# FFN layer two: outer product P7 as seven inner products, its weight differences made in layer one's first half

## The chip, the cores and the metric

One NeuronCore of a Trainium2 chip runs the whole decoder block in one launch. The metric is the device time of the launch in microseconds (us). A launch of this kernel takes about 1.9 ms; the spread of three launches was 1.7 us. Inputs and output are float32. The engines of the core are TensorE (PE in the profile), VectorE (DVE), ScalarE (ACT), GpSimd (POOL) and SyncE (SP). SP does no arithmetic here: it issues nearly all DMA transfers, one after the other, and a transfer that has to wait for its data or for a free buffer keeps those behind it from being issued.

## The reference

Only the FFN bears on the change. 2048 tokens of width 1024 go through two matrices with a squared ReLU between them:

```python
hn2 = rmsnorm(h, norm2_g)
up = jnp.einsum('bsd,df->bsf', hn2, w_up)      # 2048 x 1024 by 1024 x 4096
act = jnp.square(jax.nn.relu(up))
h = h + jnp.einsum('bsf,fd->bsd', act, w_down) # 2048 x 4096 by 4096 x 1024
return rmsnorm(h, final_g)
```

## The kernel before

**Numbers.** Operands are float32. Each one is split into a high part of type fp32r and the rest, also fp32r (`split`, L146 and L147: a copy on ACT, a subtraction on DVE), and each product is three matmuls: high by high, high by low, low by high.

**Strassen products.** Both FFN layers multiply 2x2 blocks by seven block products instead of eight (Winograd's form of Strassen's method). The seven products are called P1 to P7. Their left operands are the activations A11, A12, A22 and the sums S1 to S4 (`S3 = A11 - A21`); their right operands are weight blocks or differences of them. The four token tiles of 512 form two pairs, `PAIRS`, with index `q` 0 and 1; a product is made for both pairs.

**Layer one** (`up`) walks through 32 columns `(q, m)`, numbered 0 to 31 here: 0 to 15 are `q = 0` (the first half), 16 to 31 `q = 1`. Each column has seven slots, one for each product, of 12 matmuls (L1082), in the order P2, P6, P5, P7, P1 of the next column, P4, P3. For each slot a weight tile `hw` is split, four slots ahead of its use (`UA = 4`). The first of these needs, per column, four differences of up-weights (L919 to L922). Behind each slot, `post` evacuates the PSUM bank: it makes the activations on ACT and DVE, the sums S1 to S4 on DVE, and stores each tile to DRAM (`sd`). At column 16 the left operands of the second token pair are loaded and split, 14 tiles `sa` of 128x1024.

**Layer two** (`down`) takes the products in the order P1, P6, P7, P4, P5, P2, P3. P1, P6, P7 and P3 are outer products: eight steps over the inner dimension, each with a weight tile `wd` and one row tile `ad` per pair (L1422). P4, P5 and P2 are listed in `SPLIT`: each is itself made by seven inner products of four steps (L1249), with the two token pairs, the two halves of the inner dimension and the two halves of the columns as its 2x2 blocks. An inner step is 12 matmuls and needs one row tile; two steps share one weight tile. The rows and weights of the inner products are sums and differences:

- the row sums (`sdi`) of A22, S1 and A12 are made in layer one's second half by `inner_row` and `inner_sums`: with column `m` the row of pair 0 is loaded and subtracted, with column `m + 8` the other three sums are made (L885 to L894);
- the weight differences (`wi`) of S1 are made by the generator `weights_first` in layer one's first half: each of its 16 steps loads two quarter tiles of `w_down`, and at the next call subtracts one from the other (L988), stores the difference (`td`), and makes and stores the inner differences (L993), one per step on average. Its calls (`next(first_weights, None)`) stand in the loop over slots;
- those of A12 and A22 are made in layer two, during P1 and P7 (`more_weights`, `inner_weights`, L1137).

The tiles of `post`, of the inner sums and of `weights_first` come from one pool, `avp`, of 13 buffers of 128x512. A buffer is free again when the store that reads it has landed.

**Order.** Each engine works strictly through its own list. The code gives the dependences; the order of the list is set when the program is built, by the framework's scheduler, so that instructions of different columns are interleaved.

Of the kernel before, what the change touches and what calls it, by code (L numbers as in the profile page):

```python
# [15 lines left out]
P = 128  # L16
# [30 lines left out]
def hymba_block(ctx: ExitStack, tc: tile.TileContext, xT, gains, w_in, pool_w, w_out, w_up, w_down, out):  # L47
# [64 lines left out]
    for i in range(PAD):  # L112
# [24 lines left out]
    sdi = {i: [[dram.tile([P, 2, T], F32, name=f"sdi{i}_{n}_{c}") for c in range(4)] for n in range(4)] for i in (1, 2, 3)}  # L137
    wi = {i: {n: [dram.tile([P, 4, 256], F32, name=f"wi{i}_{n}_{c}") for c in range(2)]
              for n in ("P5", "P6", "P7", "P4")} for i in (1, 2, 3)}
    td = [[dram.tile([P, 4, 256], F32, name=f"td{i}_{c}") for c in range(8)] for i in range(2)]  # L140
# [720 lines left out]
    def up(pools, more):  # L861
# [5 lines left out]

        def inner_row(m, i):
# [10 lines left out]
        def inner_sums(m, i, t):  # L879

            rows, at = halves[i, "rows"], m % (NM // 2)
            d, r = rows[0], rows[-1]
# [96 lines left out]
        def weights_first():  # L979

            for k in range(4):
                b = {}
                for x, y in ((0, 0), (0, 1), (1, 1), (1, 0)):
                    b[x, y], t = (avp.tile([P, 2, 256], F32, tag="av", name=n) for n in ("t1", "b11"))
                    nc.sync.dma_start(t, half(w_down[0, k + 4 * x], y))
                    nc.sync.dma_start(b[x, y], half(w_down[1, k + 4 * x], y))
                    yield
                    nc.vector.tensor_tensor(b[x, y], b[x, y], t, ALU.subtract)  # L988
                    nc.sync.dma_start(half(td[0][k + 4 * x], y), b[x, y])
                    for to, one, two, p in {(0, 1): (((0, 0), (0, 1), (0, 0), "P5"),),  # L990
                                            (1, 1): (((0, 1), (1, 1), (0, 1), "P7"), ((1, 1), (1, 1), (0, 0), "P6")),
                                            (1, 0): (((1, 0), (1, 0), (1, 1), "P4"),)}.get((x, y), ()):
                        nc.vector.tensor_tensor(b[to], b[one], b[two], ALU.subtract)  # L993
                        nc.sync.dma_start(wi[S1][p][k // 2][:, 2 * (k % 2):2 * (k % 2) + 2], b[to])

        def post(q, m, s):
# [4 lines left out]
            def put(i, t, kept=None):  # L1001
                if q == 0 or m >= NM // 2 or i not in (A12, A22, S1):
                    kept = nc.sync.dma_start(sd[q][i][m // 2][:, m % 2], t)
                if q and i in (A12, A22, S1):
                    inner_sums(m, i, t)
                return kept
# [17 lines left out]
            elif s == "P6":  # L1024
                if q:
                    for i in (A22, S1, A12):
                        inner_row(m, i)
                copy("u2")
            elif s == "P7":
                copy("u3")  # L1030
# [15 lines left out]
            elif s == "P3":  # L1046
# [6 lines left out]
                put(S4, s4)  # L1053

# [13 lines left out]
        for g, (q, m, s) in enumerate(slots):  # L1068
# [4 lines left out]
            if q == 0 and (m in (1, 6, 7) or m >= NM // 2 and m % (NM // 2) not in (2, 3, 4, 5)) and s in SUMS:  # L1073
# [24 lines left out]
    def down(pools):  # L1098
        t8, s8, rs, rt, pupa, pup, rtx, rlp, tmp_, psb = pools

        SPLIT = {"P4": A22, "P5": S1, "P2": A12}
# [25 lines left out]
        source, tops = {"P4": "t2", "P5": "t1", "P2": 2}, {}  # L1127
# [21 lines left out]
        def more_weights(n, kk, w):  # L1149
# [28 lines left out]
        def make(g):  # L1178
# [11 lines left out]
            elif n == "P7":  # L1190
                w = minus(blk(b22, kk), blk(b12, kk))
# [19 lines left out]
        CHAIN = {"P1": "p1", "P6": "u2", "P7": "u3"}  # L1211
        BANKS = {"P4": {"Y": (0, 1), "Z": (2, 3), "X": (4, 5)}, "P5": {"Y": (6, 7), "Z": (2, 3), "X": (4, 5)},
# [401 lines left out]
```

## Time and profile before

| | us |
|---|---|
| median of three launches | 1913.86 (1912.65 to 1914.35) |
| profiled launch, its own time | 1917.71 |
| span of its profile | 1915.9 |
| layer one, its matmuls | about 697 to 1312 |
| layer two, its matmuls | 1312 to 1905 |

The span runs from the first to the last instruction in the trace. The profiled launch was 3.85 us above the median, and 1.8 us of it lie outside the span. "Busy" counts an engine as busy while at least one of its instructions runs; neighbours on DVE overlap a little, so a DVE operation of 128x512 that shows 0.69 us starts 0.60 us after the one before it. In a table of waits, the name on the right is what ended the wait.

### The profile page before, as it was taken

What the parts mean: (1) busy time and instruction counts of PE and PEld (TensorE: products, weight loads), DVE (VectorE), ACT (ScalarE), POOL (GpSimd) and SP (SyncE); (2) the same over time, 40 slices, a digit from 0 to 9 for tenths busy, and PEclk for the clock granted to TensorE, in tenths of its full rate; (3) what the DMA queues carried; (4) which work ended last, traced back from release to release, by engine and by line L of the source; (5) the groups of instructions that cost most, each with busy time, mean ns of one, the idle gap of its engine ahead of it and who ended that gap; (6) DMA issues with size and microseconds to landing.
All of it is one profiled execution on the core that took longest, in us unless ns stands there. A gap on an engine that the chain in (4) does not pass through costs nothing.

```text
span 1915.9 us, 26510 instructions
## 1 busy us (share of the span) xinstructions
PE 1891.8 (99%) x8995; PEld 1577.8 (82%) x8995; DVE 1424.4 (74%) x2128; ACT 1006.7 (53%) x1598; POOL 177.7 (9%) x399
## 2 busy tenths in 40 slices
PE   9999999999999999999999999999999999999997
PEld 7888888888888888788888888887888888888886
DVE  6887799667866886776787877786655547888874
ACT  5565566555554465455566555454333345656643
POOL 0211113101211030000000000000010010020120
PEclk9999999999999999999999999999999999999998
DMA  6686596787887867776777677778998889899862
GB/s 213 204 270 201 191 295 221 244 312 264 283 321 295 282 239 252 261 254 227 273 285 269 233 258 262 243 266 310 379 358 308 282 253 314 291 297 334 295 209 91
DMA packets 206034, 509.68 MB, mean 266 GB/s; under 512 B 24256, under 2 KB 30400, under 8 KB 202048
## 3 DMA queue, kind: packets, MB, share of 16 engines
q1 hardware_dynamic: 201136, 499.24, 75.1%
q0 software_dynamic: 4608, 8.39, 2.4%
q8 instruction: 73, 1.20, 0.3%
q14 instruction: 73, 0.60, 0.1%
q10 hardware_dynamic: 144, 0.26, 0.0%
HBM read 335.82 MB, written 171.97 MB: 265 GB/s over the span
## 4 chain that ended last, share of the span: by engine, by line
PE 89%; DMA 4%; DVE 4%; issue 1%; ACT 1%; POOL 0%; SPq 0%; DVEq 0%; ACTq 0%
PE pY L1082 16%; PE pb L1422 16%; PE pb L1249 12%; PE pZ L1082 8%; PE pd L178 8%; PE pd L180 8%; PE pd L179 8%; PE pX L1082 4%; PE po L675 2%; PE pta L664 1%; DMA xt<-in_xT_dram 1%; PE pr L231 1%; DMA t<-in_w_down_dram 1%; PE pm L205 1%; PE pz L617 1%; DMA wr<-in_w_down_dram 1%
## 5 line engine op out<-in xcount | busy, mean ns | idle before, releaser
L1082 PE MATMUL pY<-sa,hw 128*128 128x512 f32 x1536 | 365.7, 389 | 0.7 <-ACT u L1015 0.7
L1422 PE MATMUL pb<-ad,wd 128*128 128x512 f32 x1488 | 340.9, 390 | 1.3 <-ACT ad L146 1.2
L1082 PEld LDWEIGHTS pY<-sa,hw 128*128 128x128 f32 x1536 | 288.1, 188 | 60.9 <-ACT u L1015 1.1
L1422 PEld LDWEIGHTS pb<-ad,wd 128*128 128x128 f32 x1488 | 278.5, 188 | 60.0 <-ACT ad L146 1.6
L178 PE MATMUL pd<-h,hl 128*128 128x512 f32 x752 | 299.8, 399 | 0.7 <-DVE qkr L424 0.7
L180 PE MATMUL pd<-h,hl 128*128 128x512 f32 x752 | 296.9, 395 | 0.0
L179 PE MATMUL pd<-h,hl 128*128 128x512 f32 x752 | 296.7, 395 | 0.0
L147 DVE TENSOR_TENSOR ad<-ar,ad 128x1024 fp32r<-128x1024 f32 x148 | 179.8, 1221 | 70.2 <-ACT ad L146 70.0
L1249 PE MATMUL pb<-ad,wd 128*128 128x512 f32 x1008 | 229.2, 389 | 0.5 <-DVE ad L147 0.5
L1249 PEld LDWEIGHTS pb<-ad,wd 128*128 128x128 f32 x1008 | 189.0, 188 | 40.4 <-DVE ad L147 1.2
L146 ACT ACTIVATE ad<-ar 128x1024 fp32r<-128x1024 f32 x148 | 155.6, 1053 | 116.8 <-issue 47.6
L1082 PE MATMUL pZ<-sa,hw 128*128 128x512 f32 x768 | 186.7, 390 | 1.5 <-DVE a L1032 1.5
L1082 PEld LDWEIGHTS pZ<-sa,hw 128*128 128x128 f32 x768 | 143.9, 188 | 32.2 <-DVE a L1032 2.4
L178 PEld LDWEIGHTS pd<-h,hl 128*128 128x128 f32 x752 | 142.1, 189 | 28.2 <-DVE qkr L424 1.0
L180 PEld LDWEIGHTS pd<-h,hl 128*128 128x128 f32 x752 | 141.8, 189 | 28.0
L179 PEld LDWEIGHTS pd<-h,hl 128*128 128x128 f32 x752 | 142.0, 189 | 27.1
L146 ACT ACTIVATE hl<-raw 128x512 fp32r<-128x512 f32 x168 | 104.0, 631 | 111.2 <-PE pd L180 70.7
L147 DVE TENSOR_TENSOR hl<-raw,hl 128x512 fp32r<-128x512 f32 x168 | 114.1, 685 | 53.6 <-ACT hl L146 50.0
L147 DVE TENSOR_TENSOR hw<-rt,hw 128x512 fp32r<-128x512 f32 x128 | 86.8, 686 | 51.4 <-ACT hw L146 51.3
L1009 ACT ACTIVATE a<-a 128x512 f32<-128x512 f32 x96 | 59.5, 630 | 86.8 <-DVE a L1048 41.4
L146 ACT ACTIVATE wd<-wr 128x1024 fp32r<-128x1024 f32 x40 | 42.4, 1060 | 112.4 <-PE pb L1422 94.1
L1082 PE MATMUL pX<-sa,hw 128*128 128x512 f32 x384 | 93.1, 389 | 0.0
(219 smaller groups left out, 2652.2 us busy)
## 6 DMA issues: line engine op xcount, KB each, us to landing
ar<-sd SPq DMA_DIRECT2D x100, 512.0 KB, 5.4
wr<-in_w_down_dram SPq DMA_DIRECT2D x64, 512.0 KB, 5.4
rb<-in_w_up_dram SPq DMA_DIRECT2D x30, 1024.0 KB, 6.4
sd<-a SPq DMA_DIRECT2D x112, 256.0 KB, 4.0
raw<-in_w_in_dram SPq DMA_DIRECT2D x50, 512.0 KB, 4.5
ar<-sdi SPq DMA_DIRECT2D x48, 512.0 KB, 5.7
sd<-s SPq DMA_DIRECT2D x88, 256.0 KB, 4.0
sdi<-hr SPq DMA_DIRECT2D x72, 256.0 KB, 4.4
```

Of the source, the lines that this page charges most:

```text
L146: nc.scalar.activation(hi, src, AF.Copy)
L147: return nc.vector.tensor_tensor(lo, src, hi.bitcast(F32), ALU.subtract)
L178: nc.tensor.matmul(ps, hl[:, 0, c], hi, start=(k == 0), stop=False)
L179: nc.tensor.matmul(ps, hl[:, 0, c], lo, start=False, stop=False)
L180: mm = nc.tensor.matmul(ps, hl[:, 1, c], hi, start=False, stop=(k == n - 1))
L205: marks["pm"] = nc.tensor.matmul(pm[:, c:c + 1], ss[:, c * P:(c + 1) * P], inv[n], start=(i == 0), stop=(i == len(parts) - 1))
L231: mm = nc.tensor.matmul(pr[:, b * P:(b + 1) * P], yr[:, x, b:b + 1].to_broadcast([P, P]), identr, start=(b == 0 and x == 0), stop=(b == TB ...
L675: nc.tensor.matmul(po[:, p * 256 + to:p * 256 + to + hi - lo], vw[:, 2 * p + v], at[:, x, lo:hi], start=(p == 0 and n == 0 and x == 0), sk ...
L1009: nc.scalar.activation(t, src, AF.Relu)
L1082: nc.tensor.matmul(t, w[:, wx, c], a[:, ax, c % 2], start=first and c == 0 and x == 0, stop=last and c == G - 1 and x == 2, skip_group_che ...
L1249: nc.tensor.matmul(b, t[:, wx, 2 * (kk % 2) + c, i * P:(i + 1) * P], a[:, ax, c], start=p in ("P1", "P5", "P2") and kk == 0 and c == 0 and ...
L1422: nc.tensor.matmul(ps[q, n], block(t, wx, c, n), left_[q][:, ax, c], start=(n_ in ("P1", "P3") and kk == 0 and c == 0 and x == 0), stop=(n ...
```

## The change

P7 joins `SPLIT`. Four things follow.

1. Layer two makes P7 with seven inner products; the chain of evacuations changes with it (P6's result is copied into `u2` and `u3`, P7's is added to `u3`, and `c21` is copied from there). The PSUM banks of P4 and P5 trade places.
2. `weights_first` runs twice, first for S1 as before, then for S3 (`td[2]` and `wi[S3]`): 32 steps instead of 16. Its calls are spread anew: three in each of columns 1 to 3 as before, two in each of columns 5, 7, 9 and 11, up to five in columns 12 to 15 (before: three in 12 and 13, two in 14).
3. Layer one's second half makes the row sums of S3 too, with two buffers of `avp` for the loaded rows. In its first column the sums wait until the slot P3 is done (`waiting`).
4. The inner weights of A22 are made during P6 from the tile at hand, instead of during P7 from a tile loaded back.

```diff
@@ up
-            if m == NM // 2 - 1:
-                halves[i, "rows"] = [avp.tile([P, T], F32, tag="av", name="hr")]
-            elif m == NM - 1:
-                halves[i, "rows"].append(avp.tile([P, T], F32, tag="av", name="hr"))
-            elif m < NM // 2:
-                t = srp.tile([P, 2, T], F32, tag="sr", name="hr")
-                halves[i, "rows"] = [t[:, 0], t[:, 1]]
+            if m < NM // 2:
+                t = srp.tile([P, 2, T], F32, tag="sr", name="hr") if i != S3 else None
+                halves[i, "rows"] = [t[:, x] if t is not None else avp.tile([P, T], F32, tag="av", name="hr")
+                                     for x in range(2)]
...
+            for i, one, two, keep in ((S1, 1, 0, 0), (S3, 3, 1, 2)):
+                for k in range(4):
...
+                        nc.sync.dma_start(t, half(w_down[two, k + 4 * x], y))
+                        nc.sync.dma_start(b[x, y], half(w_down[one, k + 4 * x], y))
+                        yield
+                        nc.vector.tensor_tensor(b[x, y], b[x, y], t, ALU.subtract)
+                        if i == S1 or (x, y) != (0, 1):
+                            nc.sync.dma_start(half(td[keep][k + 4 * x], y), b[x, y])
...
-            if q == 0 and (m in (1, 6, 7) or m >= NM // 2 and m % (NM // 2) not in (2, 3, 4, 5)) and s in SUMS:
+            n = cols.index((q, m))
+            if s in (() if n == 0 else SUMS if n < 4 else ("P5", "P4") if n in (5, 7, 9, 11) else
+                     SUMS + ("P6", "P3") if 12 <= n < 16 else ()):
                 next(first_weights, None)
@@ down
-        SPLIT = {"P4": A22, "P5": S1, "P2": A12}
+        SPLIT = {"P7": S3, "P4": A22, "P5": S1, "P2": A12}
...
-                nc.sync.dma_start(td[1][kk], w)
-            elif n == "P7":
-                inner_weights(A22, kk, blk("t2", kk))
+                nc.sync.dma_start(half(td[1][kk], 0), half(w, 0))
+                if kk >= 4:
+                    nc.sync.dma_start(half(td[1][kk], 1), half(w, 1))
+                inner_weights(A22, kk, w)
...
-            elif n == "P7":
-                w = minus(blk(b22, kk), blk(b12, kk))
...
-        BANKS = {"P4": {"Y": (0, 1), "Z": (2, 3), "X": (4, 5)}, "P5": {"Y": (6, 7), "Z": (2, 3), "X": (4, 5)},
+        BANKS = {"P4": {"Y": (6, 7), "Z": (2, 3), "X": (4, 5)}, "P5": {"Y": (0, 1), "Z": (2, 3), "X": (4, 5)},
+                 "P7": {"Y": (0, 1), "Z": (2, 3), "X": (4, 5)},
...
-                if n_ == "P7":
-                    nc.scalar.activation(val("c21", q)[:, n], b, AF.Copy)
-                    add_residual(val("c21", q)[:, n], j1, 0, n)
+                if n_ == "P6":
+                    nc.scalar.activation(val("u3", q)[:, n], b, AF.Copy)
```

**What moves: PE in layer two.** Here are the first rows of the PE's list in layer two before (L1422 is an outer matmul, L1249 an inner one, `pb` the PSUM bank, `ad` a row tile, `wd` a weight tile):

```order
L1422 MATMUL pb<-ad,wd 128x512 x1152
L1249 MATMUL pb<-ad,wd 128x512 x1008
L1422 MATMUL pb<-ad,wd 128x512 x24
L205 MATMUL pm<-inv_115,ss 128x1 x4
L1422 MATMUL pb<-ad,wd 128x512 x36
```

And the same rows now, where the two lines are L1435 and L1258:

```order
L1435 MATMUL pb<-ad,wd 128x512 x768
L1258 MATMUL pb<-ad,wd 128x512 x1344
L1435 MATMUL pb<-ad,wd 128x512 x24
L205 MATMUL pm<-inv_115,ss 128x1 x4
L1435 MATMUL pb<-ad,wd 128x512 x36
```

384 outer matmuls are gone and 336 inner ones have come, 48 fewer in all.

**What moves: DVE in column 14 of layer one.** The stretch begins with the activation A22 of column 14 (L1032 before, L1038 now). `hw` is the split of a weight tile for a coming slot, `sa` that of a left operand of column 16, L919 to L922 (now L920 to L923) make up-weight differences, L988 and L993 (now L990 and L996) are `weights_first`, L1039 (now L1045) is S1. Before:

```order
L1032 TENSOR_TENSOR a_10609<-pZ,u_10607 128x512
L147 TENSOR_TENSOR hw<-rt,hw 128x512
L147 TENSOR_TENSOR sa<-sr,sa 128x1024
L147 TENSOR_TENSOR hw<-rt,hw 128x512
L993 TENSOR_TENSOR t_10533<-t_10533,t_10474 128x512
L147 TENSOR_TENSOR sa<-sr,sa 128x1024
L147 TENSOR_TENSOR hw<-rb,hw 128x512
L147 TENSOR_TENSOR sa<-sr,sa 128x1024
L147 TENSOR_TENSOR hw<-rt,hw 128x512
L1039 TENSOR_TENSOR s_10655<-a_10652,a_10609 128x512
L919 TENSOR_TENSOR rt<-rb 128x512
L921 TENSOR_TENSOR rt<-rb 128x512
```

The same stretch now:

```order
L1038 TENSOR_TENSOR a_10744<-pZ,u_10742 128x512
L990 TENSOR_TENSOR t_10658<-t_10658,b_10659 128x512
L147 TENSOR_TENSOR hw<-rb,hw 128x512
L147 TENSOR_TENSOR hw<-rt,hw 128x512
L990 TENSOR_TENSOR t_10687<-t_10687,b_10688 128x512
L920 TENSOR_TENSOR rt<-rb 128x512
L922 TENSOR_TENSOR rt<-rb 128x512
L990 TENSOR_TENSOR t_10710<-t_10710,b_10711 128x512
L147 TENSOR_TENSOR hw<-rb,hw 128x512
L1045 TENSOR_TENSOR s_10797<-a_10794,a_10744 128x512
L921 TENSOR_TENSOR rt<-rb,rt 128x512
L147 TENSOR_TENSOR hw<-rb,hw 128x512
```

Three weight subtractions stand where three operand splits stood, and the splits of column 16's operands come later in the list. From the A22 of column 13 up to and with the `hw` of column 17's slot P6, the list holds 74 rows before (60 of 128x512, 14 `sa`, among them 4 of L988 and 4 of L993) and 81 now (72 of 128x512, 9 `sa`, among them 10 of L990 and 11 of L996).

**What moves: PE at columns 16 and 17.** `pX`, `pY` and `pZ` are the PSUM banks of P2, of P1, P6, P7 and P4, and of P5 and P3. The rows begin with the slot P2 of column 16; before:

```order
L1082 MATMUL pX<-sa,hw 128x512 x12
L1082 MATMUL pY<-sa,hw 128x512 x12
L1082 MATMUL pZ<-sa,hw 128x512 x2
L1082 MATMUL pY<-sa,hw 128x512 x8
L1082 MATMUL pZ<-sa,hw 128x512 x12
L1082 MATMUL pY<-sa,hw 128x512 x4
L1082 MATMUL pZ<-sa,hw 128x512 x10
L1082 MATMUL pY<-sa,hw 128x512 x24
L1082 MATMUL pX<-sa,hw 128x512 x2
L1082 MATMUL pY<-sa,hw 128x512 x2
L1082 MATMUL pZ<-sa,hw 128x512 x2
L1082 MATMUL pX<-sa,hw 128x512 x10
```

Now:

```order
L1092 MATMUL pX<-sa,hw 128x512 x7
L1092 MATMUL pY<-sa,hw 128x512 x12
L1092 MATMUL pX<-sa,hw 128x512 x5
L1092 MATMUL pY<-sa,hw 128x512 x14
L1092 MATMUL pZ<-sa,hw 128x512 x13
L1092 MATMUL pY<-sa,hw 128x512 x10
L1092 MATMUL pZ<-sa,hw 128x512 x6
L1092 MATMUL pY<-sa,hw 128x512
L1092 MATMUL pX<-sa,hw 128x512 x2
L1092 MATMUL pZ<-sa,hw 128x512 x5
L1092 MATMUL pY<-sa,hw 128x512 x8
L1092 MATMUL pX<-sa,hw 128x512 x10
```

The slots of columns 16 and 17 are cut into smaller pieces, and slots of column 17 begin before those of column 16 are done. Between the end of column 13's slot P7 and the first matmul of column 17's slot P6 stand 255 matmuls before and 243 now.

More of the change, by code (lines that the diff above doesn't have):

```diff
@@ L1024, in post @@
             elif s == "P6":
-                if q:
-                    for i in (A22, S1, A12):
+                if q and m != NM // 2 - 1:
+                    for i in INNER:
                         inner_row(m, i)
@@ L1029, in post @@
             elif s == "P7":
+                if q and m == NM // 2 - 1:
+                    for i in INNER:
+                        inner_row(m, i)
                 copy("u3")
```

53 lines of the change are left out of this document (28 added, 25 removed).

## The prediction

> **What bounds the kernel now.** I read the page's shares first, then the waits of PE, then stretches.
>
> ```profile
> span 1915.9 us, 26510 instructions
> PE 1891.8 (99%) x8995; PEld 1577.8 (82%) x8995; DVE 1424.4 (74%) x2128; ACT 1006.7 (53%) x1598; POOL 177.7 (9%) x399
> PE 89%; DMA 4%; DVE 4%; issue 1%; ACT 1%; POOL 0%; SPq 0%; DVEq 0%; ACTq 0%
> ```
>
> PE is busy for 1891.8 of 1915.9 us, and 89% of the chain that ends last are matmuls. So a matmul taken out is time won, unless its place is filled by waiting. From the start of layer one on PE has waited little (engine, line, what it waited for: us in total, times, longest):
>
> ```profile
> PE pZ L1082 <- DVE a L1032: 1.5, 2, 1.2
> PE pb L1422 <- ACT ad L146: 1.2, 1, 1.2
> PE pr L231 <- POOL yr L1290: 0.9, 1, 0.9
> PE pY L1082 <- ACT u L1015: 0.7, 1, 0.7
> ```
>
> The change touches three stretches. The windows give their load (columns: stretch, length, PE, PEld, DVE, ACT, POOL busy with counts, granted clock, DMA share, GB/s): columns 14 to 16 of layer one with the end of 13, the rest of its second half, and in layer two P6, P7 and P4.
>
> ```profile
> 965.00:1023.00 58.00, 58.00 (x257) 48.04 (x256) 52.42 (x74) 43.05 (x68) 0.00 (x0) 1.00 0.80 288
> 1023.00:1290.00 267.00, 267.00 (x1179) 221.08 (x1179) 206.54 (x337) 141.25 (x252) 0.00 (x0) 1.00 0.74 252
> 1421.00:1508.00 87.00, 87.00 (x385) 72.03 (x385) 48.95 (x44) 28.89 (x32) 0.00 (x0) 1.00 0.88 317
> 1508.00:1594.00 86.00, 86.00 (x382) 71.19 (x380) 44.44 (x44) 37.54 (x45) 6.92 (x8) 1.00 0.86 277
> 1594.00:1670.00 76.00, 76.00 (x337) 62.94 (x336) 61.22 (x62) 45.45 (x47) 0.00 (x0) 1.00 0.86 292
> ```
>
> PE is busy throughout all five. DVE runs at 90% in the first (52.42 of 58), 77% in the second and 81% in P4: the first is where room is short.
>
> **Term 1: matmuls.** P7's outer form was 384 matmuls, its inner form is 336 (7 products by 4 steps by 12). The pace comes from a run of 24 and the start of the next:
>
> ```profile
> 960.26 5.60 PE L1082 MATMUL pY<-sa,hw 128*128 128x512 f32 x24
> 965.70 2.88 PE L1082 MATMUL pX<-sa,hw 128*128 128x512 f32 x12
> ```
>
> 5.44 us for 24 is 0.2267 us each; P4's window (337 in 76 us, 0.2255) says that the inner form keeps this pace. 48 x 0.2267 = **10.9 us saved**.
>
> **Term 2: the turn of layer one, columns 13 to 17.** `weights_first` has 16 more steps: 32 loads, 28 stores, 32 DVE operations at 0.60 us, 19.2 us of DVE in all. Where DVE runs ahead of PE they lie beneath matmuls: in columns 5 to 11 DVE had such room, 92.61 us busy of 127:
>
> ```profile
> 808.00:935.00 127.00, 127.00 (x562) 105.17 (x561) 92.61 (x149) 70.10 (x125) 0.00 (x0) 1.00 0.71 244
> 947.55 0.69 DVE L988 TENSOR_TENSOR t<-t,b 128x512 f32<-128x512 f32 x1 [4.17 <-DMA t<-in_w_down_dram]
> ```
>
> Even a wait of 4.17 us at the head of DVE's queue, with the weight splits behind it, did not stop PE there. At the turn it is different. Follow DVE from the A22 of column 13, which cannot start before PE has finished that column's P7, to the split that column 17's P6 needs:
>
> ```profile
> 966.30 0.69 DVE L1032 TENSOR_TENSOR a<-pZ,u 128x512 f32<-128x512 f32 x1 [3.14 <-ACT u L1015]
> 968.26 0.69 DVE L988 TENSOR_TENSOR t<-t,b 128x512 f32<-128x512 f32 x1 [0.67 <-DMA t<-in_w_down_dram]
> 970.14 0.69 DVE L988 TENSOR_TENSOR t<-t,b 128x512 f32<-128x512 f32 x1 [0.58 <-DMA t<-in_w_down_dram]
> 972.03 0.69 DVE L988 TENSOR_TENSOR t<-t,b 128x512 f32<-128x512 f32 x1 [0.60 <-DMA t<-in_w_down_dram]
> 984.64 0.69 DVE L988 TENSOR_TENSOR t<-t,b 128x512 f32<-128x512 f32 x1 [0.55 <-DMA t<-in_w_down_dram]
> 997.07 0.68 DVE L1048 TENSOR_TENSOR a<-pZ,u 128x512 f32<-128x512 f32 x1
> 997.67 0.68 DVE L920 TENSOR_TENSOR rt<-rb,rt 128x512 f32<-128x512 f32 x1
> 998.27 2.35 DVE L147 TENSOR_TENSOR sa<-sr,sa 128x1024 fp32r<-128x1024 f32 x2
> 1000.54 0.69 DVE L147 TENSOR_TENSOR hw<-rb,hw 128x512 fp32r<-128x512 f32 x1
> 1011.31 1.23 DVE L147 TENSOR_TENSOR sa<-sr,sa 128x1024 fp32r<-128x1024 f32 x1 [0.74 <-ACT sa L146]
> 1022.79 0.69 DVE L147 TENSOR_TENSOR hw<-rt,hw 128x512 fp32r<-128x512 f32 x1
> 1023.27 0.62 PE L1082 MATMUL pY<-sa,hw 128*128 128x512 f32 x2
> ```
>
> The rows from 997.07 to 1000.54 give the pace: 0.60 us from one start to the next, 2.27 for two `sa`. Before: 60 operations at 0.60 and 14 `sa` at 1.135 make 51.9 us of work; from 966.30 to the split's end (1023.4) are 57.1 us, so 5.2 us were waiting, 2.4 of it for four weight loads. PE had finished column 13's P7 at 965.5 (the 23rd matmul of the run at 960.26), 0.8 us before 966.30, and its 255 matmuls from there take 57.8 us: both arrive together, at 1023.3. The room of 57.8 - 0.8 - 51.9 = 5.1 us was used up by the waits, with nothing to spare.
>
> After: 72 x 0.60 + 9 x 1.135 = 53.4 us of work, against 243 x 0.2267 = 55.1 us of matmuls. The room is 55.1 - 0.8 - 53.4 = **0.9 us**. In the list the waits can only grow: ten weight loads instead of four. If other waits stay (5.2 - 2.4 = 2.8) and each load costs between nothing (landed, as DVE comes later) and 0.6, the waits are 2.8 to 8.8. Beyond that a burst's first load can cost 4.17 again, and if DVE is so late that nothing is waited for, they fall to zero. I take 4.9: the loads at half of 0.6 (3.0), and of the others 1.9, those of `sa` and stores, since the small gaps vanish when DVE lags. PE then waits 4.9 - 0.9 = **4.0 us**, between 0 and 8.8 + 4.2 - 0.9 = 12.1. The transfers themselves have room there (DMA share 0.80, 288 GB/s), and ACT too (43 of 58 us). What lies behind a waiting DVE is `hw` and `sa` for the next slots, and PE waits for these.
>
> **Term 3: layer one's second half.** S3's inner sums are 4 operations for each of 8 column pairs, 32 x 0.60 = 19.2 us; 16 loads and 32 stores of 256 KB come, 8 stores go. DVE goes from 206.5 to about 223 of 267 us (84%). Its waits there (all of them are shown) say that it is ahead, standing mostly for ACT's weight copy, which itself waits for a free buffer:
>
> ```profile
> DVE hw L147 <- ACT hw L146: 43.4, 23, 3.9
> DVE a L1032 <- ACT u L1015: 8.3, 7, 1.5
> DVE a L890 <- ACT a L1010: 5.9, 7, 1.3
> DVE hr L885 <- ACT a L1010: 2.8, 6, 1.0
> ```
>
> 43.4 us of slack cover 17 us of new work: 0 us, with a lower bound of 0 and an upper one in the second rival.
>
> **Term 4: layer two.** Inner P7 takes 28 row splits and 14 weight splits like P4, whose window held DVE at 61 of 76 us, DMA at 0.86, and PE at 100%; weight differences (8 of 128x1024) are gone from it. P6 gets A22's inner weights (16 x 0.60 = 9.6 us on 48.95 of 87: 67%), without the reload; its transfers go from 48 to 54 of 512 KB, 317 to about 353 GB/s. The nearest row with so much is P1's, where PE waited for 1.2 us at its start, already in the waits above, and then no more:
>
> ```profile
> 1350.00:1400.00 50.00, 50.00 (x223) 41.38 (x222) 29.13 (x31) 16.82 (x20) 4.64 (x6) 1.00 1.01 372
> ```
>
> So 0, from 0 to 1.2 for a new entry wait. At the entry P6's two copies per bank replace P7's two; the stall moves nowhere.
>
> **Sum.** -10.9 + 4.0 + 0 + 0 = -6.9 us. The profiled launch took 1917.71, 3.85 above the median of three, so its durations are scaled by 0.2% at most, which changes no term by 0.1. From the median: 1913.9 - 6.9 = **1907.0 us**.
>
> **The rivals.**
>
> *The turn eats the gain.* If the loads come late as a burst (the 4.17 row) and all ten cost 0.6, PE waits 12.1 us: 1913.9 - 10.9 + 12.1 = 1915.1, no change to be measured. For it: SP issues the loads in order behind stores that wait for DVE, and the pool of 13 buffers now feeds twice the steps. Against it: columns 5 to 11 take 8 steps where there was room. Chance 0.20.
>
> *Buffers run short in the second half (slower).* S3 keeps two loaded rows and one activation of `avp` over each column pair: 13 - 3 - 3 = 7 are left for a column's own seven tiles, 10 before. A tile then waits until a store has landed, and a row that is loaded into it lands later still (KB each, median us to landing, from 935 to 1030):
>
> ```profile
> hr<-sd SPq DMA_DIRECT2D x9, 256.0 KB, 6.7
> sdi<-hr SPq DMA_DIRECT2D x1, 256.0 KB, 5.1
> ```
>
> 5.1 + 6.7 = 11.8 us in a row. DVE's longest harmless wait there was 3.9, its lead is at most the four slots made ahead, 10.9 us. If every pair stops PE for 2 us, 8 x 2 = 16 us: 1907.0 + 16 = 1923. It outweighs the gain from 0.9 us per pair (6.9 / 8). For it: the pool is exactly full. Against: the sums are off PE's path, and ran without any DVE wait for a DMA in this stretch. Chance 0.13.
>
> *A long gap costs the clock as well.* At the start of the kernel gaps of 1.35 and 0.53 us within 3 us were followed by half the clock:
>
> ```profile
> 6.55 0.50 PE L469 MATMUL pd<-h,hl 128*128 128x512 f32 x1 [1.35 <-ACT h L340]
> 8.60 0.79 PE L469 MATMUL pd<-h,hl 128*128 128x512 f32 x1 [0.53 <-ACT h L340]
> 10.00:12.00 2.00, 2.00 (x6) 1.61 (x5) 2.00 (x5) 2.00 (x4) 0.00 (x0) 0.50 1.05 399
> 14.00:16.00 2.00, 2.00 (x8) 1.56 (x7) 1.90 (x4) 2.00 (x5) 0.00 (x0) 0.74 0.93 334
> 800.00:805.00 5.00, 3.84 (x17) 2.83 (x16) 4.64 (x9) 1.78 (x3) 0.00 (x0) 1.00 0.77 268
> ```
>
> From 8.6 to about 15, some 6 us at half speed, 3 us are lost: 1907.0 + 3 = 1910.0. A gap of 1.2 us in layer one (800 to 805) left the clock at 1.00, and the new order cuts the slots into pieces, so that the wait is spread. Chance 0.10. The Trainium skill ("TensorE: Matmul & The Clock Gate", section "What's actually happening") says that the array falls to half its clock after an idle window of about 3.4 us and needs as long a busy one to recover; by that, four microseconds in one piece would cost 1.7 more, an estimate from its figures, and spread ones nothing. The row at 10 to 12 us agrees on the half; that shorter gaps can lead there is this case's own.
>
> *The wait never comes:* -10.9, 1903.0. It is the near end of the forecast, not a case of its own.
>
> **How the numbers follow.** Changes of less than 0.2% (3.8 us) cannot be told from none. Forecast (wait below 7 us): 0.57, faster. Turn eats the gain: 0.20, same. Clock: 0.10, on the border, half faster, half same. Buffers: 0.13, slower. Faster 0.57 + 0.05 = 0.62, same 0.25, slower 0.13. The range runs from 1902.5 (no wait, launches 0.6 lower) to 1916.5 (the turn at its worst and a layer-two entry wait of 1.2); the buffers' case is left out. The forecast alone: 1902.5 to 1910.
>
> **What would show it.** Term 1: L1258 with 1344 matmuls, P7's window about 76 us. Term 2: waits of PE for `hw` or `sa` between 985 and 1035, some 4 us, in pieces; DVE there at 95% or more, with waits for `t<-in_w_down_dram`. Term 3: no PE wait from 1040 to 1290; DVE near 84%. DVE or ACT waiting there for stores (`sdi<-hr`, `sd<-s`) would speak for the buffers. Term 4: PE at 100% through P6, P7, P4. A time above 1910 with columns 13 to 17 clean would prove the ledger at the turn wrong; one below 1902 would mean that stalls I have not priced went away.

## The result: slower by 0.3%

| | before | after |
|---|---|---|
| median of seven launches, us | 1913.48 (1912.15 to 1914.35) | 1920.85 (1916.04 to 1922.11, and one disturbed) |
| ratio, 95% interval | 1 | 1.0032 (1.0021 to 1.0044) |
| profiled launch, its own time / span, us | 1917.71 / 1915.9 | 1916.04 / 1914.2 |
| layer one: its first matmul to layer two's first, us | 615.1 | 623.7 |
| layer two: its first matmul to the end of the span, us | 603.8 | 595.0 |

The prediction was 1907.0, faster; the time lies outside its range (1902.5 to 1916.5). One launch of the changed kernel, 2690.66 us at a mean granted clock of 0.653, was disturbed and is left out of the ratio (the median of the other six is 1919.40). The launch of after that was profiled is the fastest of its seven, and that of before is slower than all of its seven. So the two traces show where time comes and goes, but their difference is not the difference of the medians. Layer one began between 691.3 and 697.0 us in the profiles of this study, though nothing ahead of it is edited; the last two rows of the table leave that out.

The page of after, first its totals, then one line of the chain that ended last, by line and as a share of the span:

```profile
span 1914.2 us, 26732 instructions
PE 1885.2 (98%) x8947; PEld 1572.3 (82%) x8947; DVE 1481.5 (77%) x2216; ACT 1025.0 (54%) x1616; POOL 178.2 (9%) x399
PE pb L1258 16%; PE pY L1092 13%; PE pb L1435 12%; PE pZ L1092 6%; PE pd L180 4%; PE pd L178 4%; PE pd L179 4%; PE pX L1092 3%; DMA hn<-hs 2%; DMA t<-in_w_down_dram 2%; DMA sd<-a 1%; DVE hw L147 1%; PE pb L1375 1%; DMA raw<-in_w_in_dram 1%; PE pr L231 1%
```

The 48 matmuls are gone (8947 for 8995). Two loads have come into the chain with 2% each: `hn<-hs` was not on the list of before, and `t<-in_w_down_dram` had 1%. The waits of PE from layer one on (us in total, times, longest), where before had 1.5 and 1.2 in the first two rows:

```profile
PE pZ L1092 <- DVE a L1038: 6.7, 4, 3.7
PE pb L1435 <- ACT ad L146: 3.3, 1, 3.3
PE pY L1092 <- ACT u L1018: 0.7, 1, 0.7
```

Where they lie, from PE's timeline (start, us, engine, line, form, count, idle time ahead and what ended it):

```profile
801.95 3.02 PE L1092 MATMUL pZ<-sa,hw 128*128 128x512 f32 x12 [0.23 <-DVE a L1038]
844.05 5.49 PE L1092 MATMUL pZ<-sa,hw 128*128 128x512 f32 x12 [3.73 <-DVE a L1038]
885.70 3.01 PE L1092 MATMUL pZ<-sa,hw 128*128 128x512 f32 x12 [0.50 <-DVE a L1038]
926.29 3.02 PE L1092 MATMUL pZ<-sa,hw 128*128 128x512 f32 x12 [2.21 <-DVE a L1038]
1319.16 22.04 PE L1435 MATMUL pb<-ad,wd 128*128 128x512 f32 x96
1344.47 5.77 PE L1435 MATMUL pb<-ad,wd 128*128 128x512 f32 x17 [3.27 <-ACT ad L146]
1498.55 304.80 PE L1258 MATMUL pb<-ad,wd 128*128 128x512 f32 x1344
```

The first four stand ahead of the slots P3 (bank Z) of columns 4, 6, 8 and 10, the columns in which `sums_second` loads the `hs` rows; those of 6, 8 and 10 come behind a column with two calls of `weights_first`. Why column 8 loses less than 6 and 10, here and in most runs below, stays open. Behind the gap of 3.73 us the twelve matmuls took 5.49 us instead of 3.02: PE lost its clock as well. The windows (columns as in the prediction) show this, the turn, the second half of layer one, the entry of layer two and the inner P7:

```profile
830.00:850.00 20.00, 16.27 (x60) 12.92 (x59) 14.27 (x23) 7.98 (x15) 0.00 (x0) 0.83 0.76 263
965.00:1023.00 58.00, 58.00 (x258) 48.04 (x257) 55.20 (x86) 38.78 (x64) 0.00 (x0) 1.00 1.00 359
1040.00:1290.00 250.00, 250.00 (x1105) 207.07 (x1104) 211.40 (x344) 135.84 (x240) 0.00 (x0) 1.00 0.85 292
1330.00:1350.00 20.00, 16.73 (x66) 13.05 (x66) 11.32 (x13) 7.43 (x7) 0.00 (x0) 0.91 1.00 370
1498.50:1574.50 76.00, 76.00 (x337) 62.92 (x337) 57.26 (x55) 46.72 (x50) 5.26 (x6) 1.00 0.92 298
```

The turn, on which the prediction put its whole loss, is clean: PE 58.00 of 58. So is the second half, with DVE at 211.40 of 250, 85%. The inner P7 keeps its pace.

**What A22 stood behind.** P3 adds into the same bank Z from which A22 (L1038) is made, so PE cannot go on with P3 until DVE has done A22. DVE's timeline of after, from the A22 of column 5 to that of column 6 (rows between left out):

```profile
813.42 0.68 DVE L1038 TENSOR_TENSOR a<-pZ,u 128x512 f32<-128x512 f32 x1
...
819.40 0.69 DVE L990 TENSOR_TENSOR t<-t,b 128x512 f32<-128x512 f32 x1 [4.71 <-issue]
...
835.18 0.75 DVE L957 SCALAR_TENSOR_TENSOR hn<-hn,gains,rlast 128x512 f32<-128x512 f32 x1 [4.04 <-DMA hn<-hs]
...
841.32 0.75 DVE L957 SCALAR_TENSOR_TENSOR hn<-hn,gains,rlast 128x512 f32<-128x512 f32 x1 [1.08 <-DMA hn<-hs]
...
843.31 0.68 DVE L1038 TENSOR_TENSOR a<-pZ,u 128x512 f32<-128x512 f32 x1
```

From A22 to A22 are 29.9 us. The same two in before:

```profile
816.54 0.68 DVE L1032 TENSOR_TENSOR a<-pZ,u 128x512 f32<-128x512 f32 x1
...
832.25 1.42 DVE L956 SCALAR_TENSOR_TENSOR hn<-hn,gains,rlast 128x512 f32<-128x512 f32 x2 [3.72 <-DMA hn<-hs]
...
839.08 0.75 DVE L956 SCALAR_TENSOR_TENSOR hn<-hn,gains,rlast 128x512 f32<-128x512 f32 x1 [2.88 <-DMA hn<-hs]
...
841.55 0.68 DVE L1032 TENSOR_TENSOR a<-pZ,u 128x512 f32<-128x512 f32 x1
```

25.0 us. DVE waited for the rows `hs` there too, but PE did not stop:

```profile
840.81 5.38 PE L1082 MATMUL pZ<-sa,hw 128*128 128x512 f32 x23
```

If the order is that of after, the last 12 of these 23 are column 6's P3. They began 11 x 0.2267 us behind 840.81, at 843.30, and A22 was done at 842.23. So A22 had a lead of 1.1 us; coming 4.9 us later, it must stop PE for about 3.8, and the wait is 3.73. In after it first stands 4.71 us at L990, whose quarter of `w_down` SP had asked for at 813.46 (these loads landed 5.9 us or more after their issue; the profile names no other releaser), does five new operations (L990 and L996), and the rows come later as well. SP's own list shows why they do; first after, then before:

```profile
809.33 3.11 SPq L1006 DMA_DIRECT2D sd<-a  x2
813.46 0.44 SPq L988 DMA_DIRECT2D t<-in_w_down_dram  x1
829.26 1.33 SPq L956 DMA_DIRECT2D hn<-hs  x2
```

```profile
827.16 0.92 SPq L955 DMA_DIRECT2D hn<-hs  x2
```

SP issues in order, behind stores of tiles that DVE has yet to make: from 813 to 830 in after, SP waits 4.0 us for the differences of L990 and 3.2 us for those of L996, which it stores ahead of the row loads. The rows are asked for 15.8 us after the first A22 (829.26 - 813.42), before 10.6 us after it. A DVE that is late makes its own next load late.

**The account of the two traces.** Layer one is 8.6 us longer: 5.2 us of waits for A22 (6.7 - 1.5), 2.5 us of half clock behind the first long gap, and the rest in pieces too small for the rows. Layer two is 8.8 us shorter: 10.9 us of matmuls, less 2.1 us of entry wait (3.3 - 1.2) and about 1.8 us of clock behind it (17 matmuls in 5.77 us, at 0.2267 each 3.85 and the last one's tail), and 1.7 us that before lost elsewhere: 0.5 waiting for `ad` in an inner product, the rest in small pieces while PE shows as busy. In this pair of launches the two cancel. The medians are 7.4 us apart, 5.9 with the 1919.40 of six launches; the ratio gives 0.32% or 6.1 us. One reading of the difference is that the typical launch loses its clock behind the gap at column 10 too: in e1, e5 and e7 below that gap was 2.68 to 3.09 us and the clock fell each time, in e3 it was 2.47 and the clock stayed. The mean granted clock of after's six launches is 0.992 to 0.995, that of before's launches made beside e1 0.995 to 0.997, which fits but does not say where the clock fell. For after only this one launch was profiled, so it isn't shown.

### The profile page after: what moved, and what is told of

The parts are those of the page before. It is cut to its first block, busy times and chain, and to the rows that moved or that the text cites. A ratio compares the mean times of both kernels' runs of the same rounds, so it can differ in the third digit from the quotient of the medians.

```text
span 1914.2 us, 26732 instructions
## 1 busy us (share of the span) xinstructions
PE 1885.2 (98%) x8947; PEld 1572.3 (82%) x8947; DVE 1481.5 (77%) x2216; ACT 1025.0 (54%) x1616; POOL 178.2 (9%) x399
## 4 chain that ended last, share of the span: by engine, by line
PE 63%; DMA 7%; DVE 4%; issue 1%; ACT 1%; SPq 0%; POOL 0%; DVEq 0%; ACTq 0%; POOLq 0%
PE pb L1258 16%; PE pY L1092 13%; PE pb L1435 12%; PE pZ L1092 6%; PE pd L180 4%; PE pd L178 4%; PE pd L179 4%; PE pX L1092 3%; DMA hn<-hs 2%; DMA t<-in_w_down_dram 2%; DMA sd<-a 1%; DVE hw L147 1%; PE pb L1375 1%; DMA raw<-in_w_in_dram 1%; PE pr L231 1%
## 5 line engine op out<-in xcount | busy, mean ns | idle before, releaser
L1258 PE MATMUL pb<-ad,wd 128*128 128x512 f32 x1344 | 304.8, 389 | 0.0
L1258 PEld LDWEIGHTS pb<-ad,wd 128*128 128x128 f32 x1344 | 252.3, 188 | 52.3
L1435 PE MATMUL pb<-ad,wd 128*128 128x512 f32 x1104 | 255.1, 392 | 3.3 <-ACT ad L146 3.3
L1435 PEld LDWEIGHTS pb<-ad,wd 128*128 128x128 f32 x1104 | 207.7, 189 | 47.0 <-ACT ad L146 3.7
L147 DVE TENSOR_TENSOR ad<-ar,ad 128x1024 fp32r<-128x1024 f32 x160 | 194.4, 1221 | 51.9 <-ACT ad L146 51.6
L146 ACT ACTIVATE ad<-ar 128x1024 fp32r<-128x1024 f32 x160 | 168.3, 1053 | 101.4 <-issue 27.2
L147 DVE TENSOR_TENSOR hl<-raw,hl 128x512 fp32r<-128x512 f32 x168 | 114.0, 685 | 51.9 <-ACT hl L146 48.4
L147 DVE TENSOR_TENSOR hw<-rt,hw 128x512 fp32r<-128x512 f32 x128 | 86.7, 684 | 24.7 <-ACT hw L146 24.6
L147 DVE TENSOR_TENSOR wd<-wq,wd 128x1024 fp32r<-128x1024 f32 x56 | 68.5, 1223 | 45.6 <-ACT wd L146 45.6
L146 ACT ACTIVATE wd<-wq 128x1024 fp32r<-128x1024 f32 x56 | 59.4, 1061 | 79.5 <-PE pb L1258 69.1
```

Of the source, the lines that this page charges most:

```text
L146: nc.scalar.activation(hi, src, AF.Copy)
L147: return nc.vector.tensor_tensor(lo, src, hi.bitcast(F32), ALU.subtract)
L1258: nc.tensor.matmul(b, t[:, wx, 2 * (kk % 2) + c, i * P:(i + 1) * P], a[:, ax, c], start=p in ("P1", "P5", "P2") and kk == 0 and c == 0 and ...
L1435: nc.tensor.matmul(ps[q, n], block(t, wx, c, n), left_[q][:, ax, c], start=(n_ in ("P1", "P3") and kk == 0 and c == 0 and x == 0), stop=(n ...
```

## The experiments

The theory, A in the expectations: PE stops in columns 4 to 11 because A22, which P3 waits for, stands on DVE behind waits for loads, and with the second round of `weights_first` DVE comes to them later; the clock falls behind the long gaps. Its rivals: that the second round by itself costs nothing and the loss is made elsewhere (B); that the added calls cost the same wherever they stand (C); and in later runs the bank, the weight loads or the row loads alone. In the table, layer one and layer two are measured as above, in one profiled launch each, which may stand some 5 us off its kernel's median (5.4 in e7, 6.5 in e12). The runs were made in three groups (e1 to e4, e5 to e8, e9 to e12); the ratios are against the launches of before in the same group, whose medians were 1913.81, 1913.26 and 1912.85. So runs are compared by their ratios. In the edits, `...` stands for lines that are left out.

| | median, us | ratio (95%) | layer one | layer two | waits for A22 above 0.2 us |
|---|---|---|---|---|---|
| e1_weights_only | 1923.07 | 1.0045 (1.0028 to 1.0062) | 626.9 | 603.5 | 1.29, 2.99, 1.66, 2.68 |
| e2_one_round | 1905.37 | 0.9956 (0.9941 to 0.9971) | 614.6 | 595.2 | 1.31 |
| e3_no_row_sums | 1913.45 | 0.9998 (0.9988 to 1.0008) | 624.0 | 591.6 | 0.51, 3.39, 1.76, 2.47 |
| e4_calls_moved | 1906.21 | 0.9961 (0.9946 to 0.9976) | 617.3 | 594.0 | none |
| e5_third_bank | 1918.40 | 1.0023 (1.0014 to 1.0032) | 628.5 | 596.0 | 1.10, 3.72, 0.93, 3.09 |
| e6_rows_early | 1912.48 | 0.9990 (0.9980 to 1.0000) | 620.6 | 594.5 | 0.52, 0.84 |
| e7_weights_early | 1920.74 | 1.0041 (1.0029 to 1.0054) | 627.1 | 593.9 | 0.33, 1.21, 2.80, 0.70, 3.02, 0.42 |
| e8_moved_and_early | 1908.84 | 0.9977 (0.9966 to 0.9988) | 616.7 | 594.6 | none |
| e9_row_sums_behind | 1915.19 | 1.0012 (1.0002 to 1.0022) | 620.6 | 596.0 | 1.62 |
| e10_entry_queue | 1911.86 | 0.9995 (0.9986 to 1.0004) | 615.3 | 600.0 | none |
| e12_behind_and_queue | 1917.52 | 1.0019 (1.0008 to 1.0030) | 617.2 | 599.2 | none |

### One part alone: the second round of `weights_first`

The kernel before, with the second round and its calls only:

```diff
...
-            for k in range(4):
+            for i, one, two, keep in ((S1, 1, 0, 0), (S3, 3, 1, 2)):
+                for k in range(4):
...
-            if q == 0 and (m in (1, 6, 7) or m >= NM // 2 and m % (NM // 2) not in (2, 3, 4, 5)) and s in SUMS:
+            n = cols.index((q, m))
+            if s in (() if n == 0 else SUMS if n < 4 else ("P5", "P4") if n in (5, 7, 9, 11) else
+                     SUMS + ("P6", "P3") if 12 <= n < 16 else ()):
```

> The kernel before plus the second round of weights_first, at the places the change gives it; P7 stays an outer product, no row sums of S3, and what the second round stores is read by nobody. Theory A (columns 5 to 11: DVE stands for late w_down loads, in the next column for the hs rows of sums_second, so the A22 that frees bank Z comes late and PE stops, then runs at half clock): about 7 us over the kernel before, 1920, with PE waiting for A22 near columns 6 and 10 and none of it at the entry of layer two beyond 1.2. Rival B (buffers taken by S3's row sums, or their stores, cause all the loss): 1914, no gap there.

The ratio came out at 1.0045. The four waits are there, from PE's timeline:

```profile
798.85 3.02 PE L1086 MATMUL pZ<-sa,hw 128*128 128x512 f32 x12 [1.29 <-DVE a L1034]
840.22 4.49 PE L1086 MATMUL pZ<-sa,hw 128*128 128x512 f32 x12 [2.99 <-DVE a L1034]
881.88 3.02 PE L1086 MATMUL pZ<-sa,hw 128*128 128x512 f32 x12 [1.66 <-DVE a L1034]
923.37 4.59 PE L1086 MATMUL pZ<-sa,hw 128*128 128x512 f32 x12 [2.68 <-DVE a L1034]
```

No row sum of S3 and no change of layer two is needed for them. B falls: the added round alone costs 0.45%.

### The other parts without it

The changed kernel with one round and the old places of the calls. P7's inner products then read the weight differences of S1:

```diff
-            for i, one, two, keep in ((S1, 1, 0, 0), (S3, 3, 1, 2)):
+            for i, one, two, keep in ((S1, 1, 0, 0),):
...
-                    nc.sync.dma_start(w, wi[i][p][kp])
+                    nc.sync.dma_start(w, wi[S1 if i == S3 else i][p][kp])
...
```

> The changed kernel without the second round of weights_first (calls placed as before); P7's inner products read the weight differences of S1 instead of S3's. Theory A: the columns are as before, the 48 matmuls are saved, the entry of layer two still loses about 4 (3.3 of waiting and the clock after it, against 1.2 before): 1913.5 - 11 + 3 = 1905. Rival B: no better than 1912, since the row sums are still made.

1905.37, 0.44% or 8.4 us faster; layer two is 8.6 us shorter, layer one as before (614.6 against 615.1). The saving of the inner P7 is real, and the loss of layer one sits in the second round of weight differences; the entry wait is here too (2.76 us).

The two parts do not quite add up. +0.45% and -0.44% make 0.01%, and after is at +0.32%. The 0.31% between them is a little more than the 0.25% that the three intervals give together as independent errors. The traces do not show this excess: the second round lengthens layer one by 11.8 us in e1 (626.9 against 615.1) and by 9.1 from e2 to after. Where it lies stays open.

### The row sums of S3 taken out

```diff
-        INNER, waiting = (A22, S1, A12, S3), []
+        INNER, waiting = (A22, S1, A12), []
...
```

> The changed kernel without the row sums of S3; P7's inner products read those of S1. If the entry of layer two is late because S3's last sums and stores stand ahead of the row loads: the wait there is back at about 1.2 and the time 3 to 4 us under the changed kernel, 1915 to 1916, while the gap near column 6 stays. If the entry is late for another reason (more weights, the clock): as the changed kernel, 1917 to 1922.

1913.45, lower than expected, and 0.34% or 6.5 us below after by the ratios. The waits for A22 stayed (3.39 us the longest); what went was the entry wait. PE's first run of layer two and the loads of P1's third and fourth step on SP, in after and then here:

```profile
1319.16 22.04 PE L1435 MATMUL pb<-ad,wd 128*128 128x512 f32 x96
1337.30 5.83 SPq L1206 DMA_DIRECT2D ar<-sd  x4
```

```profile
1318.89 41.34 PE L1435 MATMUL pb<-ad,wd 128*128 128x512 f32 x179
1332.97 6.67 SPq L1206 DMA_DIRECT2D ar<-sd  x4
```

With S3's row sums and their stores in the program, the loads go out 18.1 us after layer two's first matmul, without them 14.1 us, and PE runs through. In before it was 15.6 us, with a wait of 1.17:

```profile
1327.71 6.70 SPq L1197 DMA_DIRECT2D ar<-sd  x4
```

So the entry wait is the other part of what the change costs: layer two here takes 591.6 us, 3.4 less than after's. The edit takes away the sums on DVE and their stores on SP together, so which of the two delays the loads is not separated. The other 3 us of the difference are not in these two traces, whose layers one are alike (624.0 and 623.7).

### The same calls at other places

```diff
-            if s in (() if n == 0 else SUMS if n < 4 else ("P5", "P4") if n in (5, 7, 9, 11) else
+            if s in (() if n == 0 else SUMS + ("P6", "P3") if n == 1 else SUMS + ("P6",) if n < 4 else
                      SUMS + ("P6", "P3") if 12 <= n < 16 else ()):
```

> The changed kernel with no calls of weights_first in columns 5 to 11: five in column 1, four in 2 and 3, up to five in 12 to 15. Theory A: the gaps near columns 6 and 10 go, and if the turn at columns 14 to 17 still holds, 6 to 8 us under the changed kernel, about 1911 to 1912. Rival C (DVE has too much to do wherever the steps stand): a gap opens elsewhere in layer one and the time stays at 1917 to 1922.

1906.21, 0.39% faster than before and 5 us less than expected. All the work of the change is in it; of the eight calls of columns 5, 7, 9 and 11, four are made in columns 1 to 3 and four in columns 12 to 15. PE's waits from layer one's start to its turn, those above 0.2 us:

```profile
803.77 2.57 PE L1092 MATMUL pX<-sa,hw 128*128 128x512 f32 x10 [1.09 <-DVE hw L147]
815.40 3.01 PE L1092 MATMUL pZ<-sa,hw 128*128 128x512 f32 x12 [0.91 <-DVE a L1054]
1009.55 1.66 PE L1092 MATMUL pZ<-sa,hw 128*128 128x512 f32 x6 [0.51 <-DVE sa L147]
```

From the A22 of column 5 to the next are 21.1 us here (817.92 to 838.97), and the rows are asked for 9.2 us after the first (827.08 on SP). C falls: it is not the number of calls but that they stand among the columns with the second pair's row sums. Of all kernels that do the whole computation, this one has the lowest ratio, and it beats before and after; against e8 below the intervals overlap.

### A third bank Z

PE might have wanted a free bank for the next column's P5, and not the one that A22 reads:

```diff
-                ps[q, m, bank] = psu.tile([P, T], F32, tag=bank, name="p" + bank)
+                ps[q, m, bank] = psu.tile([P, T], F32, tag=bank, name="p" + bank, bufs=3 if bank == "Z" else 2)
...
```

> The changed kernel with three PSUM banks for Z (P5 and P3) instead of two, the fourth tag R having one. If PE stands near columns 6, 8 and 10 because the next P5 has no free bank until DVE has made A22: the gaps fall below 1.5 us each, no half clock, 1912 to 1914. If DVE is simply late with everything: the same gaps under a wait for a weight split, 1917 to 1922.

The waits stayed, 3.72 and 3.09 us the longest, both with the clock lost behind them (5.47 and 4.61 us for twelve). No free bank is missing; it is the bank in use, to which P3 may not add until A22 has been read from it.

### Each of the two loads earlier

First the `hs` rows: the first two loads of each set are issued in slot P4 of the column before.

```diff
...
+            if n in (3, 5, 7, 9) and s == "P4":
+                sums_second((n + 1) // 2 - 2, None)
```

With `None`, `sums_second` only issues the two loads; the sums take the rows up when their turn comes.

> The changed kernel with the first two hs loads of sums_second in columns 4, 6, 8 and 10 issued two slots earlier (in the slot P4 of the column before). If the gap needs both waits of DVE, for w_down in the odd column and for hs in the even one: DVE's wait of 4.0 for hn near 835 falls below 1, PE's gap of 3.7 with it, no half clock, 1911 to 1914. If the wait for w_down is enough: the gap stays, 1917 to 1922.

1912.48, 0.42% below after by the ratios. The two longest of PE's waits in columns 4 to 11:

```profile
835.21 3.03 PE L1102 MATMUL pY<-sa,hw 128*128 128x512 f32 x12 [1.00 <-ACT u L1026]
878.39 3.02 PE L1102 MATMUL pZ<-sa,hw 128*128 128x512 f32 x12 [0.84 <-DVE a L1046]
```

Where after waited for 3.73 us nothing above 1.0 is left. From the A22 of column 5 to the next are 26.0 us (814.18 to 840.17); DVE takes up a set of rows without a wait 6.3 us after they were asked for (812.93 on SP, 819.19 on DVE). This takes away the long waits and their clock, not the whole loss: layer one is still 5.5 us longer than before's, 2.7 of it in PE's waits (4.9 us, none above 1.0, against 2.2) and 2.8 while PE shows as busy (615.8 against 612.9), whose cause stays open.

Then the quarters of `w_down`, loaded one call earlier in steps 8 to 17:

```diff
...
+                b[x, y], t = ahead_ or fetch(g)
+                ahead_ = fetch(g + 1) if 8 <= g < 18 else None
                 yield
...
```

> The changed kernel with the w_down loads of the steps in columns 5 to 11 issued one call earlier, two buffers of avp more. If late w_down loads start the trouble: DVE's waits of 4.4 to 4.7 at L990 there vanish, PE's gaps fall below 1.5 us each, 1911 to 1914. If avp's 13 buffers bound these columns: waits for stores take their place and the time stays at 1917 to 1922 or grows.

1920.74, as slow as after. DVE's wait for the weights near 816 us fell from 4.71 to 1.43 us, and then it stood longer for the rows:

```profile
833.50 0.75 DVE L957 SCALAR_TENSOR_TENSOR hn<-hn,gains,rlast 128x512 f32<-128x512 f32 x1 [4.89 <-DMA hn<-hs]
841.17 0.68 DVE L1045 TENSOR_TENSOR a<-pZ,u 128x512 f32<-128x512 f32 x1
```

From A22 to A22 are 28.8 us, 1.1 less than after, and PE's wait at column 6 fell by about as much, from 3.73 to 2.80; at column 10 it grew, from 2.21 to 3.02. The rows' issue on SP moved by only 1.1 us against A22 (14.7 us behind it). So theory A needs its second half sharpened: the last link is the late issue of the `hs` rows; a shorter wait for weights is mostly spent by waiting for them.

### Both remedies together

```diff
...
-            if s in (() if n == 0 else SUMS if n < 4 else ("P5", "P4") if n in (5, 7, 9, 11) else
+            if n in (3, 5, 7, 9) and s == "P4":
+                sums_second((n + 1) // 2 - 2, None)
+            if s in (() if n == 0 else SUMS + ("P6", "P3") if n == 1 else SUMS + ("P6",) if n < 4 else
                      SUMS + ("P6", "P3") if 12 <= n < 16 else ()):
```

> The calls moved as in e4 and the hs loads early as in e6. Left over in e4 were gaps of 1.1 and 0.9 us near columns 4 and 5, and 2.25 at the entry of layer two. If the hs wait makes the first two: 1904 to 1905, 1 to 2 us under e4. The entry stays, since the row sums stay.

A miss: 1908.84, no better than e4 alone (the intervals of the two ratios overlap). No wait is left in columns 4 to 11, but three of about 0.9 us came at the turn (1008 to 1012 us), for splits.

### Another place for the waiting operations

```diff
-            if q == 0 and 2 <= m < 6 and s in SUMS:
-                sums_second(m - 2, SUMS.index(s))
...
             post(q, m, s)
+            if q == 0 and 2 <= m < 6 and s in ("P7", "P4", "P3"):
+                sums_second(m - 2, ("P7", "P4", "P3").index(s))
```

> The changed kernel, with the second row sums of columns 4, 6, 8 and 10 called behind the evacuation of the slots P7, P4 and P3 instead of ahead of the matmuls of three others, so that in DVE's list the A22 of these columns stands ahead of the first operation that waits for hs rows. All loads and all DVE work stay. Theory A (PE stops because A22, which frees bank Z for the same column's P3, stands behind DVE's waits for loads): DVE goes on waiting for rows, but PE's waits for A22 in columns 6 and 10 fall from 3.7 and 2.2 us to under 1.5, the clock stays at 1.00, the wait at layer two's entry stays about 3 us; 1912 to 1915. Rival (DVE is simply late by its waits, with whatever comes next): PE waits for the weight splits hw instead, by 2 to 4 us at the same columns; 1917 to 1922.

1915.19, 0.20% below after by the ratios, just outside what A said. DVE waited for the rows even longer (28.3 us in all, 20.2 in after), and PE's waits for A22 fell from 6.7 us to 1.6. What is left of them, and what came back under other names:

```profile
859.49 4.62 PE L1090 MATMUL pZ<-sa,hw 128*128 128x512 f32 x19 [1.62 <-DVE a L1038]
871.16 2.14 PE L1090 MATMUL pX<-sa,hw 128*128 128x512 f32 x8 [1.16 <-DVE hw L147]
972.05 3.04 PE L1090 MATMUL pY<-sa,hw 128*128 128x512 f32 x12 [2.17 <-ACT u L1018]
```

So order on DVE decides which wait reaches PE, as A says, and the lateness of DVE itself is spread over the next ones, as its rival says; each is partly right.

### The entry's loads on another queue

e4_calls_moved still waits 2.25 us at layer two's entry. On top of it:

```diff
-                    last[0] = nc.sync.dma_start(rows[q], sd[q][i][kk])
+                    last[0] = (nc.scalar if g in (2, 3) else nc.sync).dma_start(rows[q], sd[q][i][kk])
```

> The kernel of e4_calls_moved, with the row loads of P1's third and fourth step issued on ACT's DMA queue instead of SP's. Theory (the wait at layer two's entry comes from SP's queue, in which these loads stand behind the stores of S3's inner rows): the loads go out earlier and the entry wait falls from 2.25 us to under 1.2; 1904 to 1905.5. Rival (the rows are late for another reason: the transfers themselves, or a free buffer): the wait stays at 2 us or more; 1906.

A miss the other way: the wait grew to 6.78 us, and layer two to 600.0. ACT's timeline:

```profile
1325.27 1.06 ACT L146 ACTIVATE wd<-wr 128x1024 fp32r<-128x1024 f32 x1 [2.89 <-DMA wr<-in_w_down_dram]
1325.30 9.16 ACTq L1206 DMA_DIRECT2D ar<-sd  x4
1334.50 1.06 ACT L146 ACTIVATE ad<-ar 128x1024 fp32r<-128x1024 f32 x1 [8.17 <-DMA ar<-sd]
```

The row of the loads spans two pairs. They now stand in ACT's list, behind a weight split that itself waits for a load from SP. The third step's pair goes out 18.4 us after layer two's first matmul (1306.86), in e4 16.7 us. The fourth step's pair goes out only at 1333.51, and ACT's next row split stands behind it: it comes 9.2 us after the first pair's issue, in e4 6.4. So the edit only changed the list in which the loads wait, and made ACT's splits wait with them. It does not tell whether SP's stores alone are to blame; e3 shows no more than that S3's row sums and stores together are to blame.

The last run puts e9's edit on top of this one.

> The kernel of e10_entry_queue, with the second row sums placed as in e9_row_sums_behind. If each of the two edits takes away a wait of its own, no wait of PE above 1 us is left from column 4 to layer two's end: 1903 to 1905. If what is left in e4_calls_moved hides elsewhere (DVE at the turn takes up what columns 4 to 11 leave): 1905 to 1908.

In columns 5 to 11 PE no longer waits (145.00 us busy of the 145 from 790), and the turn takes the time instead: `[2.47 <-DVE sa L147]` at 1008.48 us. Layer one takes what it took in e4 (617.2 against 617.3), and layer two keeps e10's loss (599.2). The second reading, that DVE's lateness moves on to the turn, held; its time did not: 1917.52. It left out the entry, which costs 5.2 us against e4 in layer two (599.2 and 594.0). The profiled launch is 6.5 us under the median, so what the other launches lose besides is not in this trace.

## Why the prediction was wrong

**Bound.** Right. A matmul taken out is time won, unless its place is filled by waiting; it was filled.

**Term 1, -10.9 us.** Right. The 1344 inner matmuls of after run at 0.2267 us each (304.64 us from the first to the next outer one), and layer two is 8.6 us shorter in e2, with an entry wait that is 1.6 us longer than before's.

**Term 2, the turn, +4.0 us. This step failed, and in two ways.** The turn itself cost nothing. DVE was busy 55.20 of 58 us there, its waits vanished (0.5 us from 985 to 1030), and PE did not stop. The prediction had named that case ("if DVE is so late that nothing is waited for, they fall to zero") and did not take it.

The other way is the costly one. The step said that in columns 5 to 11 "DVE had such room, 92.61 us busy of 127", and set the eight steps there at nothing. A busy share over seven columns is not room at the one place that matters: between the A22 of column 5 and that of column 6 DVE already stood for `hs` rows, with 1.1 us to spare, and the next 4.9 us were too many. Set at nothing, these steps cost 5.2 us of waits for A22 and 2.5 us of clock in the trace of after. The row brought as proof, a wait of 4.17 us that "did not stop PE there", is at 947.55 us, just ahead of the A22 of column 12, where no rows of the second pair are loaded. The prediction even quoted PE's wait for A22 in before, 1.2 us at 805 us, two columns ahead of where it became 3.7, listed it among PE's small waits and used it for the clock. The ledger followed the splits that PE waits for; the bank that P3 adds to was not in it.

**Term 3, the second half, 0 us.** Right: PE 250.00 of 250, DVE 85% against the 84% foreseen. The rival in which buffers run short there had the right sign, but its mechanism did not occur: PE never stopped in that stretch, and e1, which has none of those sums, is slower as well.

**Term 4, layer two, 0 us, at most 1.2 for the entry.** Right within P6, P7 and P4; too small at the entry. The wait became 3.3 us and cost the clock, together 3.9 us more than before; the bound was the old wait, taken from a list in which SP had fewer stores to issue. The stores of Term 3's sums were counted for DVE and not for SP.

**The clock.** The rival of a long gap was a part of what happened rather than another case: at 844 us and at the entry the clock fell. The Trainium skill ("TensorE: Matmul & The Clock Gate", section "What's actually happening") puts the idle window at about 3.4 us, by which the gaps of e1 would have cost no clock; there 2.68 us were enough (923.37 above; the granted clock is 0.66 from 923 to 928). The measurement decides: the shorter figure holds for this kernel.

**The two signs that the prediction named** were both there: the time came out above 1910 "with columns 13 to 17 clean", which by its own words proves the ledger at the turn wrong.

## What to carry to other kernels

Before work is put on an engine "where it has room", find the operations on it whose result the bounding engine waits for soonest, among them those that read a bank which will be added to again, and measure the lead at each of them; a busy share over a longer stretch hides the one place where a wait for a load has already used it up. Do not put two operations that wait for loads one behind the other ahead of such a read: here the same calls in other columns made the kernel 0.39% faster instead of 0.32% slower. On a queue that issues in order, count added stores against the loads behind them, above all where one stage hands over to the next.

## What was not expected of the hardware

In layer one, gaps of PE up to 2.21 us left the next twelve matmuls at 3.01 to 3.06 us, and every gap from 2.68 us on (2.68, 2.80, 2.99, 3.02, 3.09, 3.39, 3.72, 3.73) was followed by a slower twelve: 4.49 to 4.62 us behind the gaps up to 3.39, 5.47 and 5.49 behind the two longest, 1.5 to 2.5 us more. At 2.47 us both occurred: 3.01 us for twelve in e3, and in e12 6.98 us for 23, which take 5.4 at full pace. So in this stage a wait of three microseconds cost four and a half or more.
